# Placing the hi/lo splits of expert weights by an estimated landing time, in a two-layer decoder with a routed expert layer in each

## The chip, the core and the metric

The kernel runs on one core of one Trainium2 chip. The metric is device time in microseconds, from start to end of one launch; lower is better. The core's engines are TensorE (PE, with its weight loads as PEld), VectorE (DVE), ScalarE (ACT), GpSimd (POOL) and SyncE (SP). Each works through its own queue of instructions in order and waits on semaphores for the others. Data comes from device memory over 16 DMA engines; here SP issues nearly all of the weight loads.

## The reference, cut to what matters

A decoder trunk of two layers on one sequence of 1024 tokens, width 1024, in float32. Layer 0 mixes tokens with a gated DeltaNet, layer 1 with differential attention. After each mixer comes a layer norm and a hierarchical mixture of 32 experts, of which each token uses two:

```python
def expert_block(args):
    xb, e = args
    hcat = xb @ w13[e]
    hid = jax.nn.silu(hcat[:, :EXPERT_FF]) * hcat[:, EXPERT_FF:]
    return hid @ w2[e]

y_rows = lax.map(expert_block, (x_rows, block_eid)).reshape(n_rows, d)
y = jax.ops.segment_sum(y_rows * row_gate[:, None], row_tok, num_segments=n)
```

`w13[e]` is 1024 x 1024 and `w2[e]` 512 x 1024, so an expert has 8 + 4 weight tiles of 128 x 1024 floats, 512 KB each.

## The kernel before, in words

**Experts by rank.** After routing, the experts are ranked by how many rows they have. A table of capacities (`CAPS`) says, when the program is written, how many rows each rank gets; `blocks_of` (L1494) cuts them into blocks of at most 128 rows. `ORDER` says in which order the ranks are worked. In layer 0 large ranks (80 to 128 rows, one block) alternate with small ones (48 to 64 rows). In layer 1 a few ranks are large: rank 3 has three blocks (128, 128 and 96 rows), rank 4 three, ranks 5, 6 and 7 two each, and between them stand runs of ranks with only 16 to 32 rows.

**Two ways to multiply.** A block of at most 64 rows ("whole") multiplies the raw float32 weight tile as it is. A larger block uses three products of a high and a low part: of each weight tile, ACT makes the high part `mh` (a rounding copy) and DVE the low part `ml` (raw minus `mh`), in `cut_one` (L1426). Such a pair is called a split below; C3.0 is the split of tile 0 of rank 3. Layer 0 has 180 splits (15 ranks with 12 tiles), layer 1 has 120 (10 ranks). The matmuls of a tile need its `mh` and, from the second one on, its `ml`.

**The order of the work.** `plan` (L1500) writes out the steps of a layer: the eight tiles of the first product of a rank (`m1`), with the transposes of the next rank's rows (`trx`) and the second product of the rank before (`trh`, `m2`, and then `out`) put in between; `act` is silu times the other half. Where the next rank has three blocks, its transposes and the whole second product of the rank before it stand ahead of its first `m1`. `seq` is the order in which weight tiles are used. `experts` (L1561) walks through the steps. PE, ACT and DVE are each wrapped in `InOrder` (L202), so in each of these queues the instructions stand in the order in which `experts` writes them. A transposed group lands in PSUM (`mtr`, two buffers), and ACT and DVE empty it to `xT`, hi and lo.

**Loads.** `Weights` (L1375) keeps a ring of raw tiles, 22 in layer 0 and 20 in layer 1 (13 or 11, and 9 late ones). `load` (L1439) has SP issue loads in the order of `seq` as far as the ring goes; a slot is free again once the tile is split, or, for a tile that a small block also uses or that is not split, once its matmuls are done.

**Where a split is written.** Each `use(rank, i)` (L1474), called right in front of a tile's matmuls, writes splits for the tiles that come up in `seq`, as far as `AHEAD` = 9 tiles past the next one, at most one new one at a time, and loads in between. `cut` (L1465) stops when `room` (L1457) says that the `NHI` = 6 pairs of `mh` and `ml` are taken. Nothing asks whether a tile's load will have landed when ACT comes to its split. For rank 3 of layer 1 this gives, in front of the step m1(27.5) and around it:

```
m1(27.4) C3.0 C3.1 m2(28) out(28) C3.2
m1(27.5) C3.3
m1(27.6) trx(3, block 0) C3.4
m1(27.7) act(27) trx(3, block 1) trh(27) trx(3, block 2) C3.5 m2(27) out(27)
m1(3.0) ...
```

Ranks 4, 5 and 6 look alike: the first two to five splits of the rank stand in front of the small rank's `out` and of the emptying of the large rank's transposes.

Of the kernel before, what the change touches and what calls it, by code (L numbers as in the profile page):

```python
# [20 lines left out]
D = 1024  # L21
# [20 lines left out]

NRAW, NKEPT, NLATE, NHI, AHEAD = (13, 11), 5, 9, 6, 9
NATIVE = ((0,), ())
XB = (2, 3)
RAWA = 4
FIXED = 3
# [173 lines left out]
def mm3(c, out, ah, al, bh, bl, first, last, engine=None):  # L221
    mm = (engine or c.nc.tensor).matmul
    mm(out, ah, bh, start=first, stop=False)  # L223
    mm(out, ah, bl, start=False, stop=False)  # L224
    mm(out, al, bh, start=False, stop=last)  # L225
# [1149 lines left out]
class Weights:  # L1375
# [5 lines left out]
    def __init__(self, c, layer, kept, raw, seq):  # L1381
# [7 lines left out]
        self.loaded = self.split = self.free = self.spares = 0  # L1389
        self.cut_rows = [any(m > 64 for m in blocks_of(layer, r)) and r not in NATIVE[layer] for r, _ in seq]  # L1390
        self.held = [not cut or any(m <= 64 for m in blocks_of(layer, r)) for cut, (r, _) in zip(self.cut_rows, seq)]
# [4 lines left out]
        self.extra = NKEPT - 2 - (3 if layer == 0 else 0)  # L1396
        self.tiles, self.ids = {}, {}

    def expert(self, rank):
        if rank not in self.ids:  # L1400
            c = self.c
            self.ids[rank] = rank if rank < FIXED else c.nc.sync.value_load(
                c.eid[0:1, rank:rank + 1], min_val=0, max_val=NE - 1)
        return self.ids[rank]
# [34 lines left out]
    def load(self, upto):  # L1439
        while self.loaded < min(upto, len(self.ring)):  # L1440
            if self.late is None and self.loaded >= self.nearly:
                return
            if self.loaded >= self.nraw:
                before = self.ring[self.loaded - self.nraw]
                if before >= (self.free if self.held[before] else self.split):
                    return
            r, i = self.seq[self.ring[self.loaded]]
            self.tiles[r, i] = (self.load_one(self.expert(r), i),)
            self.loaded += 1

    def load_fixed(self):
# [13 lines left out]
    def cut(self, upto):  # L1465
        while self.split < upto and self.tiles.get(self.seq[self.split] if self.split < len(self.seq) else None):
            if self.cut_rows[self.split]:
                if not self.room():
                    return
                key = self.seq[self.split]  # L1470
                self.tiles[key] += self.cut_one(self.tiles[key][0])
            self.split += 1

    def use(self, rank, i):  # L1474

        p = self.seq.index((rank, i))
        while True:
            at = self.split
            self.load(len(self.seq))
            self.cut(min(p + 1 + AHEAD, at + 1))  # L1480
            if self.split == at:
                break
        self.load(len(self.seq))
        assert self.split > p, (rank, i)
        return self.tiles[rank, i]
# [8 lines left out]
def blocks_of(layer, rank):  # L1494


    return [min(P, CAPS[layer][rank] - q) for q in range(0, CAPS[layer][rank], P)]
# [63 lines left out]
def experts(c, layer, h_dram, y_dram):  # L1561
    nc, tc, ins, w = c.nc, c.tc, c.ins, c.w
    pe, act_, dve = (InOrder(tc, e) for e in (nc.tensor, nc.scalar, nc.vector))
    w.act, w.dve = act_, dve
    why = "expert and column numbers come from the one-hot tables made on chip"
    with ExitStack() as es:
# [7 lines left out]
        def block(xcol, ycol, rows, native=False):  # L1574
            b = B()
            b.native, b.at = native, 0
            b.xcol, b.ycol, b.rows = xcol, ycol, rows

            b.ways = 4 if rows <= 32 else 2
            b.cols = P // b.ways  # L1580
            b.whole = rows <= 64
            b.X = c.X[nx[0] % len(c.X)]
            nx[0] += 1
            c.last_gather = instruction(nc.gpsimd.indirect_dma_start(  # L1584
                out=b.X[0:rows], out_offset=None, in_=h_dram,
                in_offset=bass.IndirectOffsetOnAxis(ap=xcol[0:rows], axis=0), bounds_check=T - 1, oob_is_err=False))
            return b

        def acc():
            return ps.tile([P, 2, 512], F32, name="acc", bufs=3)  # L1590
# [19 lines left out]
        def trx(b):  # L1610

            if b.whole:
                n = b.cols
                b.x = xp.tile([P, KT, n], F32, tag="xTw", name=f"xTw{n}", bufs=3)
                pt = ps.tile([P, KT, n], F32, tag="mtr", name=f"mtw{n}")
                for k in range(KT):
                    pe.transpose(pt[:, k], b.X[0:n, k * P:(k + 1) * P], c.ident[0:n, 0:n])
                dve.tensor_copy(b.x, pt)
                return True
            if not b.at:  # L1620
                shape, dt = ([P, KT, b.rows], F32) if b.native else ([P, KT, 2 * P], F32R)
                b.x = xp.tile(shape, dt, tag="xT", name="xT", bufs=XB[layer])
            g = slice(4 * b.at, 4 * b.at + 4)
            (plain if b.native else turn)(b, b.X[:, b.at * 512:(b.at + 1) * 512], 4, b.x[:, g])
            b.at += 1
            return b.at == 2

        def product(b, out, x, wt, first, last):
            R = b.rows
            for half in range(2):  # L1630
                f = slice(half * 512, (half + 1) * 512)
                if b.native:
                    pe.matmul(out[0:R, half], x, wt[0][:, f], start=first, stop=last)
                    continue
                mm3(c, out[0:R, half], x[:, 0:R], x[:, R:2 * R], wt[1][:, f], wt[2][:, f], first, last, pe)
# [47 lines left out]

        def m1(bs, k, wt):
            for b in bs:
                if k == 0:
                    b.hc = acc()
                if not b.whole:
                    product(b, b.hc, b.x[:, k], wt, k == 0, k == KT - 1)
                    continue  # L1690

                wv = wt[0].rearrange("p (a h f) -> p h a f", a=2, h=b.ways)
                o = b.hc[:, 0, 0:D // b.ways].rearrange("p (a f) -> p a f", a=2)
                for h in range(b.ways):
                    pe.matmul(o[b.cols * h:b.cols * (h + 1)], b.x[:, k], wv[:, h], start=(k == 0), stop=(k == KT - 1))

        def m2(b, k, wt):
            if k == 0:
                b.py = acc()
            if not b.whole:  # L1700
                product(b, b.py, b.h[:, k], wt, k == 0, k == 3)
                return
            n, w = b.cols, D // b.ways
            i, g = k % (4 // b.ways), k // (4 // b.ways)
            x = b.h[:, i, n * g:n * (g + 1)]
            for f in range(b.ways):
                pe.matmul(b.py[n * f:n * (f + 1), 0, 0:w], x, wt[0][:, w * f:w * (f + 1)],
                          start=(k == 0), stop=(k == 3))

        blocks = {}  # L1710
# [1 line left out]
        def gather(n):  # L1712
            if n < len(c.jobs):
                r, rows = c.jobs[n]
                blocks[r] = [block(c.xidx[:, r * 8 + q:r * 8 + q + 1], c.yidx[:, r * 8 + q:r * 8 + q + 1], m,
                                   r in NATIVE[layer])
                             for q, m in enumerate(rows)]
# [7 lines left out]
        for what, j, k in c.steps:  # L1725
            r = j[0]
            if what == "m1":
                wt = w.use(r, k)
                m1(blocks[r], k, wt)
                w.done(r, k)  # L1730
            elif what == "trh":
                trh(blocks[r][0])
            elif what == "m2":
                bs = blocks[r]
                wts = [w.use(r, KT + i) for i in range(4)]
                for q, b in enumerate(bs):
                    for i in range(4):
                        m2(b, i, wts[i])
                        if b is bs[-1]:
                            w.done(r, KT + i)  # L1740
                        if i == 1 and q + 1 < len(bs):
                            trh(bs[q + 1])
                    out(b)
            elif what == "trx":
                for _ in range(2):
                    at = turned.get(r, 0)
                    if at < len(blocks[r]):
                        turned[r] = at + trx(blocks[r][at])
            elif what == "gather":
                gather(k)  # L1750
            else:
                for b in blocks[r]:
                    act(b)
# [11 lines left out]
        if c.overflow:  # L1765
# [3 lines left out]
            with tc.For_i(0, trips, 1) as it:  # L1769
# [8 lines left out]
                b = block(xc, yc, P)  # L1778
# [3 lines left out]
                for k in range(KT + 4):  # L1782
# [3 lines left out]
                    wt = (raws[k],) + w.cut_one(raws[k])  # L1786
# [147 lines left out]
```

## Time and profile before

| | us |
|---|---|
| median of 3 runs | 2745.63 |
| lowest and highest run | 2743.77, 2754.32 |
| the profiled execution, its own time | 2752.11 |
| its span in the trace | 2750.3 |

The profiled execution is 6.5 us above the median, inside the range of the runs; 1.8 us of it lie outside the span. Expert layer 0 takes about 800 to 1355 us of the span, expert layer 1 about 2117 to 2682 us. Busy times of engines are shares of a stretch. A matmul's end is modelled, so a busy PE is not a PE at its peak. The DMA share is the mean over 16 engines; in the busiest stretches of this trace it reads 1.03. The granted clock is a share of TensorE's full speed.

### The profile page before, as it was taken

What the parts mean: (1) busy time and instruction counts of PE and PEld (TensorE: products, weight loads), DVE (VectorE), ACT (ScalarE), POOL (GpSimd) and SP (SyncE); (2) the same over time, 40 slices, a digit from 0 to 9 for tenths busy, and PEclk for the clock granted to TensorE, in tenths of its full rate; (3) what the DMA queues carried; (4) which work ended last, traced back from release to release, by engine and by line L of the source; (5) the groups of instructions that cost most, each with busy time, mean ns of one, the idle gap of its engine ahead of it and who ended that gap; (6) DMA issues with size and microseconds to landing.
All of it is one profiled execution on the core that took longest, in us unless ns stands there. A gap on an engine that the chain in (4) does not pass through costs nothing. (4 is left out here: it accounts for less than half of the span.)

```text
span 2750.3 us, 40132 instructions
## 1 busy us (share of the span) xinstructions
PE 2366.5 (86%) x14447; PEld 1645.2 (60%) x14447; DVE 1503.0 (55%) x2710; ACT 1214.9 (44%) x2187; POOL 545.2 (20%) x445
## 2 busy tenths in 40 slices
PE   8999999998979989898649999999886796779990
PEld 5777777776745544444238777777664373455560
DVE  4555555564556555455295667667535422334467
ACT  5355555543325444444255555556332322223454
POOL 3333333331212111010042111111012111111104
PEclk9999999999979999999859999999987898899995
DMA  4111111124678999999951110101445969799995
GB/s 145 51 59 51 55 59 47 58 75 123 242 274 302 394 388 381 383 380 384 351 210 35 39 33 31 39 26 61 155 170 210 393 250 363 288 381 362 362 366 230
DMA packets 195484, 564.09 MB, mean 205 GB/s; under 512 B 40400, under 2 KB 63184, under 8 KB 193232
## 3 DMA queue, kind: packets, MB, share of 16 engines
q1 hardware_dynamic: 178240, 515.07, 51.0%
q0 software_dynamic: 15168, 43.01, 4.5%
q10 hardware_dynamic: 1872, 3.40, 0.4%
q8 instruction: 115, 1.88, 0.3%
q14 instruction: 89, 0.73, 0.1%
HBM read 515.58 MB, written 52.89 MB: 207 GB/s over the span
## 5 line engine op out<-in xcount | busy, mean ns | idle before, releaser
L210 DVE TENSOR_TENSOR ml<-mraw,mh 128x1024 fp32r<-128x1024 f32 x300 | 357.0, 1222 | 289.4 <-ACT mh L210 270.5
L210 ACT CAST mh<-mraw 128x1024 fp32r<-128x1024 f32 x300 | 306.7, 1052 | 281.7 <-DMA mraw<-in_w 226.1
L210 PE MATMUL acc<-mh,xT 128*128 128x512 f32 (+5 forms) x976 | 331.8, 409 | 1.6 <-ACT mh L210 1.6
L210 PE MATMUL acc<-mraw,xTw 128*32 128x256 f32 (+1 forms) x1632 | 241.4, 500 | 18.7 <-DVE xTw L210 10.1
L185 POOL TENSOR_TENSOR wl<-raw,wh 128x512 fp32r<-128x512 f32 x106 | 155.0, 1482 | 485.1 <-ACT wh L184 420.9
L210 PEld LDWEIGHTS acc<-mh,xT 128*128 128x128 f32 (+5 forms) x976 | 168.4, 173 | 88.3 <-issue 17.1
L223 PE MATMUL pj<-xh,wh 128*128 128x512 f32 x512 | 218.2, 426 | 0.0
L224 PE MATMUL pj<-xl,wh 128*128 128x512 f32 x512 | 209.6, 409 | 0.0
L225 PE MATMUL pj<-xh,wl 128*128 128x512 f32 x512 | 207.9, 406 | 0.4 <-POOL wl L185 0.4
L1584 POOL DMA_INDIRECT X<-h,xidx x69 | 71.0, 1029 | 651.1 <-PE mtw L210 339.0
L210 PE MATMUL acc<-ml,xT 128*128 128x512 f32 (+5 forms) x496 | 198.4, 404 | 0.8 <-DVE ml L210 0.8
L223 PE MATMUL pj<-hT,wh 128*128 128x512 f32 (+1 forms) x432 | 164.8, 381 | 9.1 <-DVE kll L1010 5.7
L224 PE MATMUL pj<-hT,wh 128*128 128x512 f32 (+1 forms) x432 | 166.9, 386 | 0.0
L225 PE MATMUL pj<-hT,wl 128*128 128x512 f32 (+1 forms) x432 | 161.2, 373 | 2.1 <-POOL wl L185 2.1
L210 PE MATMUL acc<-mh,hT 128*128 128x512 f32 (+5 forms) x480 | 158.4, 401 | 0.1
L210 PE MATMUL acc<-mraw,hTw 128*32 128x256 f32 (+1 forms) x816 | 129.3, 540 | 30.4 <-ACT hTw L210 23.9
L210 PEld LDWEIGHTS acc<-mraw,xTw 128*32 128x32 f32 (+1 forms) x1632 | 71.4, 124 | 127.8 <-issue 71.2
L408 DVE SCALAR_TENSOR_TENSOR cv<-pr,cw,cv 128x512 f32<-128x512 f32 x144 | 119.0, 826 | 51.2 <-ACT cv L405 49.1
L1114 ACT ACTIVATE e<-sc,sm 128x256 f32<-128x256 f32 (+7 forms) x128 | 94.6, 742 | 89.7 <-DVE sm L1112 89.3
L225 PEld LDWEIGHTS pj<-xh,wl 128*128 128x128 f32 x512 | 97.2, 190 | 20.1 <-POOL wl L185 0.9
L210 PEld LDWEIGHTS acc<-mh,hT 128*128 128x128 f32 (+5 forms) x480 | 82.2, 172 | 44.6 <-issue 10.5
L224 PEld LDWEIGHTS pj<-xl,wh 128*128 128x128 f32 x512 | 97.7, 191 | 18.1 <-issue 1.7
(407 smaller groups left out, 4917.7 us busy)
## 6 DMA issues: line engine op xcount, KB each, us to landing
mraw<-in_w SPq DMA_DIRECT2D x720, 512.0 KB, 10.7
raw<-in_w_in SPq DMA_DIRECT2D x32, 512.0 KB, 3.7
yin<-y SPq DMA_DIRECT2D x16, 1024.0 KB, 6.9
raw<-in_w_kvq SPq DMA_DIRECT2D x21, 512.0 KB, 3.6
h<-res SPq DMA_DIRECT2D x16, 512.0 KB, 3.9
p<-ores POOLq DMA_DIRECT2D x12, 512.0 KB, 4.8
res<-p SPq DMA_DIRECT2D x12, 512.0 KB, 5.8
mh<-in_w SPq DMA_DIRECT2D x12, 512.0 KB, 8.1
```

The source lines that it names most:

```text
L185: c.nc.gpsimd.tensor_tensor(l[:, s], src[:, s], h[:, s].bitcast(F32), OP.subtract)
L210: out = getattr(self.engine, name)(*args, **kwargs)
L223: mm(out, ah, bh, start=first, stop=False)
L224: mm(out, ah, bl, start=False, stop=False)
L225: mm(out, al, bh, start=False, stop=last)
L408: nc.vector.scalar_tensor_tensor(a, pr[:, 1 + j:513 + j], cw[:, idx, j:j + 1], a, op0=OP.mult, op1=OP.add)
L1114: nc.scalar.activation(e[:, 0:L], st[m][:, 0:L], AF.Exp, bias=sm[:, 2 + m:3 + m], scale=SC, accum_out=sm[:, 4 + m:5 + m])
L1584: c.last_gather = instruction(nc.gpsimd.indirect_dma_start(out=b.X[0:rows], out_offset=None, in_=h_dram, in_offset=bass.IndirectOffsetOnAx ...
```

## The change

`Weights` gets a clock of its own, `now`, kept while the program is written. Each matmul group of a block adds a constant (0.45, 0.9 or 1.45 by its rows, 1.7 for the one rank that multiplies natively), each transposed group 0.8. Each load gets an estimated landing time, `land`: 1.4 after the one before it, or after `now`, whichever is later. When a tile is used, `now` is moved up to its `land`. A split is then written only if its tile's estimated landing is not later than `now`, or if it is the split of the tile in use or of the next one (`must`). The loads, the ring, the six pairs and the steps stay as they are. The renaming of `w` to `z` in `m2` is needed because `w` is now read there.

```diff
+CLOAD, CSLICE, CTURN = 1.4, {32: 0.45, 64: 0.9, 128: 1.45}, 0.8
...
+        self.now = self.loads = self.must = 0
+        self.land = {}
...
             self.tiles[r, i] = (self.load_one(self.expert(r), i),)
+            if self.now:
+                self.loads = max(self.loads, self.now) + CLOAD
+            self.land[self.ring[self.loaded]] = self.loads
             self.loaded += 1
...
     def cut(self, upto):
...
-                if not self.room():
+                if not self.room() or self.split > self.must and self.land.get(self.split, 0) > self.now:
                     return
...
         p = self.seq.index((rank, i))
+        self.must = p + 1
+        self.now = max(self.now, self.land.get(p, 0))
         while True:
...
+        def cost(b):
+            return 1.7 if b.native else CSLICE[32 if b.rows <= 32 else 64 if b.rows <= 64 else 128]
...
         def m1(bs, k, wt):
             for b in bs:
+                w.now += cost(b)
...
         def m2(b, k, wt):
+            w.now += cost(b)
...
-            n, w = b.cols, D // b.ways
+            n, z = b.cols, D // b.ways
...
                     if at < len(blocks[r]):
+                        w.now += CTURN
                         turned[r] = at + trx(blocks[r][at])
```

Followed through by hand, the new rule leaves 156 of the 300 splits where they were, writes 144 later (92 in layer 0, all among ranks 7 to 15; 52 in layer 1, among ranks 3 to 7) and none earlier. For rank 3 of layer 1 it gives:

```
m1(27.4) m2(28) out(28)
m1(27.5)
m1(27.6) trx(3, block 0)
m1(27.7) act(27) trx(3, block 1) trh(27) trx(3, block 2) C3.0 m2(27) out(27) C3.1
m1(3.0) C3.2 C3.3 ...
```

Rank 4 is the same. For rank 5 the splits C5.0 and C5.1 now stand behind all of its transposes, in front of m1(19.6), and for rank 6 C6.0 in front of m1(16.7).

## Rows read from the trace of the kernel before

**Rows 1.** Stages: us; busy PE, PEld, DVE, ACT, POOL (count); clock, DMA share, GB/s.

```profile
850.00:1350.00 500.00, 455.68 (x2076) 239.13 (x2073) 258.53 (x279) 212.79 (x277) 60.30 (x55) 0.97 1.02 384
...
2220.00:2280.00 60.00, 58.44 (x463) 40.35 (x461) 14.55 (x23) 11.96 (x21) 7.79 (x8) 1.00 0.60 222
2320.00:2380.00 60.00, 60.00 (x387) 36.81 (x383) 14.89 (x21) 13.15 (x21) 5.78 (x6) 0.98 0.66 235
2400.00:2460.00 60.00, 57.08 (x471) 40.31 (x472) 20.36 (x30) 16.29 (x28) 7.80 (x8) 0.94 0.99 378
2480.00:2660.00 180.00, 177.83 (x847) 107.05 (x846) 99.07 (x107) 82.24 (x107) 20.44 (x18) 1.00 0.98 374
```

**Rows 2.** Waits, 2080 to 2700 us: total us, times, longest.

```profile
PE mtr L210 <- DVE xT L210: 52.1, 4, 14.5
...
ACT mh L210 <- DMA mraw<-in_w: 70.9, 22, 17.2
```

**Rows 3.** First stall, timeline: start, us, engine, line, operation, tiles, count [idle before <-releaser].

```profile
2186.60 1.08 PE L210 MATMUL acc<-mraw,xTw 128*32 128x256 f32 x8
...
2191.35 1.04 ACT L210 CAST mh<-mraw 128x1024 fp32r<-128x1024 f32 x1 [17.24 <-DMA mraw<-in_w]
2192.42 1.23 DVE L210 TENSOR_TENSOR ml<-mraw,mh 128x1024 fp32r<-128x1024 f32 x1 [19.85 <-ACT mh L210]
...
2197.85 1.07 ACT L210 CAST xT<-mtr 128x512 fp32r<-128x512 f32 x2
...
2200.05 1.97 PE L210 MATMUL mtr<-ct_all,X 128*128 128x128 f32 x8 [12.37 <-DVE xT L210]
...
2208.51 0.80 PE L210 MATMUL acc<-mh,xT 128*128 128x512 f32 x1
```

**Rows 4.** Stages: the four stalls, from the last matmul before to the next transposes.

```profile
2187.68:2200.05 12.37, 0.00 (x1) 0.00 (x1) 6.40 (x8) 6.81 (x10) 1.03 (x2) 0.50 1.03 403
2299.33:2312.75 13.42, 0.00 (x0) 0.00 (x1) 6.40 (x8) 6.81 (x10) 1.47 (x2) 0.59 1.03 402
2390.90:2402.72 11.82, 0.01 (x2) 0.00 (x0) 7.71 (x9) 6.93 (x9) 1.23 (x2) 0.62 1.03 398
2461.64:2476.10 14.46, 0.00 (x1) 0.00 (x1) 7.72 (x9) 6.93 (x9) 1.74 (x3) 0.63 1.03 408
```

**Rows 5.** Timeline, stalls two to four: the rank's first split and its first matmul.

```profile
2304.24 1.04 ACT L210 CAST mh<-mraw 128x1024 fp32r<-128x1024 f32 x1 [16.61 <-DMA mraw<-in_w]
...
2320.78 0.80 PE L210 MATMUL acc<-mh,xT 128*128 128x512 f32 x1
...
2392.42 1.04 ACT L210 CAST mh<-mraw 128x1024 fp32r<-128x1024 f32 x1 [9.49 <-DMA mraw<-in_w]
...
2406.49 0.80 PE L210 MATMUL acc<-mh,xT 128*128 128x512 f32 x1
...
2464.87 1.04 ACT L210 CAST mh<-mraw 128x1024 fp32r<-128x1024 f32 x1 [7.68 <-DMA mraw<-in_w]
...
2479.43 0.50 PE L210 MATMUL acc<-mh,xT 128*128 128x512 f32 x1
```

**Rows 6.** Timeline, end of layer 1: last weight loads, a late split, last matmuls.

```profile
2561.66 97.99 SPq L1423 DMA_DIRECT2D mraw<-in_w  x70
...
2590.96 1.05 ACT L210 CAST mh<-mraw 128x1024 fp32r<-128x1024 f32 x1 [3.46 <-DMA mraw<-in_w]
...
2680.20 1.93 PE L210 MATMUL acc<-mraw,hTw 128*32 128x256 f32 x32 [0.35 <-ACT hTw L210]
```

**Rows 7.** Layer 0, 1050 to 1300 us: DMA issues (KB, us to landing), then SP's waits.

```profile
mraw<-in_w SPq DMA_DIRECT2D x168, 512.0 KB, 12.0
...
SPq L1423 <- DMA mraw<-in_w: 156.9, 168, 2.7
```

**Rows 8.** Timeline, end of layer 0: last weight loads, last matmuls.

```profile
1331.61 12.69 SPq L1423 DMA_DIRECT2D mraw<-in_w  x10
...
1351.97 3.76 PE L210 MATMUL acc<-mraw,hTw 128*64 128x512 f32 x16 [0.52 <-ACT hTw L210]
```

More of the change, by code (lines that the diff above doesn't have):

```diff
@@ L1706, in m2 @@
             for f in range(b.ways):
-                pe.matmul(b.py[n * f:n * (f + 1), 0, 0:w], x, wt[0][:, w * f:w * (f + 1)],
+                pe.matmul(b.py[n * f:n * (f + 1), 0, 0:z], x, wt[0][:, z * f:z * (f + 1)],
                           start=(k == 0), stop=(k == 3))
```

## The prediction, made before the changed kernel had run

> **What bounds the kernel now.** I read the profile page first. Its slices show DMA and TensorE both near full in the two expert layers, so the page does not say which of them a split can hold up; the change moves nothing outside those layers. So I cut them into stages.
>
> Layer 0 is bound by DMA: from 850 to 1350 us the DMA share is 1.02 without a break [rows 1]. SP issued 168 weight loads in 250 us of that stretch, and in front of 168 it waited for an earlier load, not for a free ring slot [rows 7]. The layer also ends with its loads: the last ten were issued between 1331.6 and 1344.3 us, a load takes 12.0 us to land, and the last matmuls start at 1352.0 [rows 7, 8].
>
> Layer 1 changes its bound from stage to stage. While ranks 3 and 4 are multiplied, PE is full and the DMA share falls to 0.60 and 0.66, because loads wait for PE to free slots; from 2400 to 2460 us DMA is at 0.99; from 2480 to 2660 both are nearly full [rows 1].
>
> Then the waits. In layer 1, PE waited four times, 52.1 us together, for DVE to empty `mtr` into `xT` [rows 2]. The timeline of the first stall shows why: ACT stood 17.24 us in front of C3.0, whose load landed at 2191.35, and the `xT` copies, whose input had been in PSUM since about 2186.6, came behind it in ACT's queue, at 2197.85. PE went on at 2200.05 [rows 3]. The four stalls last 12.37, 13.42, 11.82 and 14.46 us, 52.07 in all, which is the wait's total; in each, PE does nothing and DMA runs at 1.03 [rows 4].
>
> **The change, part by part.** It removes and adds no instruction: 300 casts, 300 subtractions and all loads stay. SP's loads keep their order; POOL's queue holds no split. What moves are 144 splits, one ACT and one DVE instruction each, later in those two queues. The estimate itself costs the chip nothing, since it runs while the program is written.
>
> Layer 0: 92 splits move, all among ranks 7 to 15. I count 0. What hides them is the DMA stream: with the share at 1.02, an earlier matmul only meets a load that has not landed, and the last three ranks have no splits, so the end stays tied to the last load. If a late split held a ring slot too long, loads would be late next; the slower rival prices that. The bounds are a gain of 3 us (the last matmuls against the last landing give no more [rows 7, 8]) and that loss.
>
> Layer 1, stalls: with C3.0 behind the emptying of rank 3's transposes, PE can start the next transposes when the first ones are emptied. From the first `xT` cast to PE's next transposes took 2.2 us in the trace; about 1.1 of it lies beside the small rank's last matmuls (1.08 us) [rows 3]. So I leave 1.0 us of each stall. What PE did from the end of a stall to the large rank's first matmul stays, at the same durations, as the granted clock is low there either way (0.50 to 0.63, so mostly at 1.2 GHz) [rows 4]. But that matmul also needs its split: landing plus 1.04 on ACT plus 1.23 on DVE, some 2.3 us [rows 3]. The four first matmuls [rows 3 to 5]:
>
> - Rank 3: 2187.68 + 1.0 + (2208.51 - 2200.05) = 2197.1; the split allows 2193.7. 11.4 us earlier.
> - Rank 4: 2299.33 + 1.0 + (2320.78 - 2312.75) = 2308.4; the split allows 2306.5. 12.4 us earlier.
> - Rank 5: 2390.90 + 1.0 + (2406.49 - 2402.72) = 2395.7; the split allows 2394.7. 10.8 us earlier.
> - Rank 6: 2461.64 + 1.0 + (2479.43 - 2476.10) = 2466.0; the split allows 2467.2. 12.2 us earlier.
>
> How much of that reaches the end depends on DMA. A gain on PE lasts only if the loads behind it come earlier too, and they do where DMA had gaps that a slot freed earlier closes. With 1.03 as full, the gaps are 60 x (1 - 0.60/1.03) = 25 us behind stall 1, 22 behind stall 2, 2.3 behind stall 3 and 180 x (1 - 0.98/1.03) = 8.7 behind stall 4 [rows 1]. So stalls 1 and 2 count in full, 11.4 and 12.4. Stall 3 counts 2.3, since PE just reaches the next unlanded load sooner. For stall 4 PE is the bound to the end: loads ended at 2659.7 plus some 12 us of landing, the last matmuls start at 2680.2 [rows 6, 7]. It has 8.7 us of gaps plus that lead of some 8 us, more than 12.2. Against it, the splits of ranks 8 to 11 do not move, and one there already waited 3.46 us for its load [rows 6]; with PE earlier, such waits grow. Between 8.7 (gaps alone) and 12.2 I take 10.
>
> New waits: a large rank's splits now come one or two tiles ahead instead of up to nine. Its loads follow each other faster than PE uses tiles of two or three blocks, and PE is full in these stages [rows 1]; a split takes 2.3 us in two engines that are at most 55% busy there. I count 0, at worst one split per moved rank, 5 x 2.3 = 11.5 us in layer 1. Behind a split that still waits on ACT stand the small rank's `out` copies and its silu; only the accumulators wait for those.
>
> Sum: 11.4 + 12.4 + 2.3 + 10 = 36.1 us. The profiled execution took 2752.1 us, 6.5 above the median; 2752.1 becomes 2716.0, and the median 2745.6 becomes 2709.5.
>
> **A rule against it.** The trace shows DMA at 1.03 in all four stalls [rows 4]. The Trainium skill, page Perfetto Trace Analysis, section Identifying the Most-Contended Engine, says that the engine (or memory traffic) with the highest use in a regime is the one to work on first. Applied to the stalls, that is DMA, which this change does not touch, and the sum would be 0. My sum goes by the stage behind each stall instead, where DMA falls to 0.60 and 0.66 [rows 1], and so counts full stalls only there.
>
> **Rivals.**
>
> *A: the wait only changes its name.* PE would wait for the loads themselves. For it: DMA is full in every stall. Against it: C3.0's load had landed 17 us before rank 3's first matmul [rows 3], and DMA has gaps soon after. It would give at most stall 3's kind of gain once, 2.3 us: 2743.3. This is also where the page's rule leads.
>
> *B: the estimate is too early.* The change then does only part of what it says: where `land` runs ahead of the real landings, splits again stand in front of copies that could go first. For ranks 3 and 4 the rule puts no split ahead of the transposes, whatever the real landing, so stalls 1 and 2 go anyway. For ranks 5 to 7 it rests on the estimate. With stalls 1 and 2 alone: 2745.6 - 23.8 = 2721.8.
>
> *C, slower: late splits keep ring slots.* Place: ranks 8 to 15 of layer 0, with the small ranks between them 192 loads at 250/168 = 1.49 us, 286 us [rows 7]. A slot of the 22 must be free 22 x 1.49 = 32.7 us after its issue, or 20.7 after landing. Moved splits come at most 11 tile steps later, 16.4 us, so this should not bite. If a slot were held 24 us, the ring would turn in 36 us instead of 32.7: 10% of 286, 29 us. Layer 1's ring is two slots smaller and its gain would go the same way: 2745.6 + 29 = 2775. It decides from 20.7 us between landing and split.
>
> **How the numbers follow.** About 0.5%, 13.7 us, is what a measurement of this kernel can tell from no change. My forecast has 0.71; it lies between 24 us of gain with some loss and all four stalls in full (46.8 us, 2698.8). B has 0.15, A 0.09, C 0.05. Faster takes the forecast and B: 0.86. Same is A: 0.09. Slower is C: 0.05. The range goes from 2697, all four stalls and 2 us of layer 0, to 2732, B with 10 us of new split waits. A and C lie outside it, 14 in 100.
>
> **What would show it.** Right: in the changed kernel's layer 1 the wait of PE's `mtr` for DVE's `xT` falls from 52 us to under 8; ACT's casts wait for loads less than the 70.9 us of before [rows 2]; rank 3's first matmul comes about 11 us and rank 4's about 24 us earlier, counted from the start of layer 1; DMA's stages at 0.60 and 0.66 come sooner and are shorter. Layer 0 keeps its length within 3 us and its DMA share of 1.02. Wrong: the same 50 us appear as waits of PE's matmuls for `mraw` loads (A); stalls 3 and 4 remain (B); SP waits for DVE or PE instead of earlier loads in layer 0 and the DMA share falls under 1 (C).

## The result, and the profile after

The changed kernel took 2703.53 us (median of 4 runs, 2701.77 to 2706.94) against 2746.6 us (4 runs) for the kernel before: ratio 0.9842, 95% interval 0.9828 to 0.9855. That is 43.1 us less; the prediction had 36.1 less and a range of 2697 to 2732.

The two profiled executions differ by 45.2 us of span. Cut at the first and last matmul of each expert layer (first-matmul times of the timeline, subtracted):

| part of the span, us | before | after | difference |
|---|---|---|---|
| up to layer 0's first expert matmul | 801.5 | 800.2 | -1.3 |
| layer 0, first to last expert matmul | 550.5 | 545.6 | -4.8 |
| between the layers | 765.6 | 767.0 | +1.3 |
| layer 1, first to last expert matmul | 562.6 | 522.0 | -40.6 |
| behind it | 70.1 | 70.3 | +0.2 |

Layer 1 is where the time came from. Its waits in the changed kernel, 2080 to 2720 us (total us, times, longest), to be held against [rows 2]:

```profile
ACT mh L212 <- DMA mraw<-in_w: 46.4, 32, 7.2
...
PE acc L212 <- DMA mraw<-in_w: 16.4, 28, 1.8
...
PE acc L212 <- DVE ml L212: 2.8, 4, 0.8
...
PE mtr L212 <- DVE xT L212: 1.6, 3, 1.1
```

The wait of `mtr` for `xT` is gone (52.1 us before, 1.6 now). It did not become a wait for loads: PE's matmuls waited 14.8 us for `mraw` in the same stretch of the kernel before and wait 16.4 us now. ACT still waits for loads, more often but shortly (7.2 us at the longest, 17.2 before), and PE waited only 1.7 us for a high part.

The place of the first stall, timeline of the changed kernel, the counterpart of [rows 3]:

```profile
2182.13 1.08 PE L212 MATMUL acc<-mraw,xTw 128*32 128x256 f32 x8
...
2183.14 1.74 PE L212 MATMUL mtr<-ct_all,X 128*128 128x128 f32 x8
...
2187.73 1.06 ACT L212 CAST mh<-mraw 128x1024 fp32r<-128x1024 f32 x1
...
2189.08 0.49 PE L212 MATMUL acc<-mh,xT 128*128 128x512 f32 x1
```

The transposes now follow the small rank's last matmuls at once, where PE stood 12.37 us before [rows 4]. The split (2187.73) stands behind all emptying and finds its load landed: no idle time is noted in front of it. The next first matmuls and the last matmuls:

```profile
2112.83 1.97 PE L212 MATMUL acc<-mh,xTw 128*64 128x512 f32 x4 [0.78 <-DVE xTw L212]
...
2285.06 1.05 ACT L212 CAST mh<-mraw 128x1024 fp32r<-128x1024 f32 x1 [1.51 <-DMA mraw<-in_w]
...
2286.16 0.51 PE L212 MATMUL acc<-mh,xT 128*128 128x512 f32 x1
...
2359.57 0.51 PE L212 MATMUL acc<-mh,xT 128*128 128x512 f32 x1 [1.18 <-ACT mh L212]
...
2430.80 0.50 PE L212 MATMUL acc<-mh,xT 128*128 128x512 f32 x1 [0.57 <-ACT mh L212]
...
2634.85 1.93 PE L212 MATMUL acc<-mraw,hTw 128*32 128x256 f32 x32 [0.35 <-ACT hTw L212]
```

The first row is the layer's first matmul, from which everything below is counted (before, it stood at 2117.59); then come the first matmuls of ranks 4, 5 and 6. At rank 4 the split waited 1.51 us for its load, at ranks 5 and 6 PE waited 1.18 and 0.57 us for the split: the first loads of these ranks are the next limit. The stages of the changed kernel (columns as in [rows 1]):

```profile
2183.14:2189.08 5.94, 4.75 (x54) 3.28 (x50) 3.29 (x7) 3.52 (x7) 2.04 (x3) 0.88 1.03 400
2220.00:2260.00 40.00, 38.69 (x368) 25.54 (x366) 9.42 (x18) 7.74 (x17) 6.76 (x7) 1.00 0.75 277
2300.00:2340.00 40.00, 40.00 (x236) 24.95 (x238) 10.73 (x14) 9.06 (x13) 4.00 (x4) 1.00 0.81 311
2340.00:2620.00 280.00, 263.15 (x1580) 159.66 (x1576) 139.76 (x162) 118.51 (x165) 36.72 (x35) 0.98 1.02 396
...
850.00:1350.00 500.00, 455.03 (x2072) 232.18 (x2070) 256.82 (x278) 212.76 (x278) 63.06 (x55) 0.99 1.02 384
```

The second and third rows hold the gaps of DMA behind stalls 1 and 2: 0.75 and 0.81 over 40 us, against 0.60 and 0.66 over 60 us before [rows 1]. Read in steps of 10 us, DMA stood below 0.95 from 2220 to 2270 and from 2320 to 2380 us, and now does so only between 2220 and 2250 and between 2320 and 2340. From 2340 us on it is full. The queue that issues loads says the same. SP's waits, 2080 to 2720 us, before:

```profile
SPq L1423 <- PE acc L210: 183.9, 103, 15.8
SPq L1423 <- DMA mraw<-in_w: 161.6, 186, 3.5
```

and after:

```profile
SPq L1428 <- DMA mraw<-in_w: 234.4, 260, 2.8
SPq L1428 <- PE acc L212: 79.7, 64, 14.2
```

Loads that waited for PE to free a slot now wait for the loads ahead of them. In layer 0 (last row of the stages) nothing of the kind moved: DMA share 1.02 as before.

### The profile page after: what moved, and what is told of

Same layout as the page of the kernel before. It is cut to its first block, busy times and chain, and to the rows that moved or that the text cites. A ratio compares the mean times of both kernels' runs of the same rounds, so it can differ in the third digit from the quotient of the medians.

```text
span 2705.1 us, 40128 instructions
## 1 busy us (share of the span) xinstructions
PE 2366.5 (87%) x14447; PEld 1636.9 (61%) x14447; DVE 1503.5 (56%) x2710; ACT 1214.4 (45%) x2187; POOL 548.1 (20%) x445
## 5 line engine op out<-in xcount | busy, mean ns | idle before, releaser
L212 PE MATMUL acc<-mraw,hTw 128*32 128x256 f32 (+1 forms) x816 | 122.7, 515 | 13.9 <-ACT hTw L212 7.2
L212 PEld LDWEIGHTS acc<-ml,xT 128*128 128x128 f32 (+5 forms) x496 | 84.9, 171 | 52.7 <-DVE ml L212 25.4
L212 PEld LDWEIGHTS acc<-mh,hT 128*128 128x128 f32 (+5 forms) x480 | 82.3, 173 | 54.8 <-ACT mh L212 12.4
```

The source lines that it names most:

```text
L212: out = getattr(self.engine, name)(*args, **kwargs)
```

## The experiments

Each is the changed kernel with one edit to the condition in `cut` (and `self.layer` kept for it), or a kernel with one constant changed. Below, g stands for `self.split > self.must and self.land.get(self.split, 0) > self.now`. Ratios are against the kernel before, run beside them, with 95% intervals. "L1" is layer 1 from its first to its last matmul (562.6 us before, 522.0 after), "rank 3 at" the first matmul of rank 3 counted from the same start, from one profiled execution each.

**One layer alone.** The rule is applied in layer 1 only, then in layer 0 only.

```diff
-                if not self.room() or g:
+                if not self.room() or self.layer == 1 and g:
```

> The estimate gates splits in layer 1 alone; layer 0 is as in the kernel before. Theory (the gain is the four stalls of layer 1; the 6 us by which layer 0 ended earlier in the trace of the changed kernel come from a higher granted clock in its first 60 us, before any moved split, and not from the change): as fast as the changed kernel within 3 us, 2701 to 2707, ratio to before 0.983 to 0.986. Rival (layer 0's 92 moved splits give some 6 us): 2708 to 2711.

2702.3 us, ratio 0.9836 [0.9822, 0.9851]; L1 521.8.

```diff
+                if not self.room() or self.layer == 0 and g:
```

> The estimate gates splits in layer 0 alone; layer 1 is as in the kernel before. Theory: no change, within 3 us of the kernel before, 2743 to 2750, ratio 0.999 to 1.001. Rival (layer 0 gains): 2739 to 2742, ratio 0.998 or less.

2746.35 us, ratio 1.0 [0.999, 1.0009]; L1 563.2. Its wait of `mtr` in layer 1:

```profile
PE mtr L212 <- DVE xT L212: 54.7, 4, 15.0
```

Layer 1 alone gives all of the gain; the 92 splits moved in layer 0 give nothing. The 4.8 us by which layer 0 was shorter in the profile after are not the rule's: the second kernel, with the rule in layer 0, needs 550.5 us there as before; the first, without it, 546.7. What went along with the length was the granted clock in the layer's first 60 us: before,

```profile
800.00:860.00 60.00, 57.51 (x204) 32.12 (x205) 29.80 (x31) 28.82 (x36) 7.03 (x6) 0.89 0.59 206
```

the rule in layer 0 only,

```profile
800.00:860.00 60.00, 57.54 (x206) 31.49 (x206) 32.03 (x33) 30.07 (x37) 9.07 (x6) 0.91 0.59 208
```

the rule in layer 1 only,

```profile
800.00:860.00 60.00, 56.77 (x223) 29.77 (x221) 34.76 (x37) 31.39 (x39) 11.13 (x5) 0.99 0.62 221
```

and 0.98 in the profile after. Two executions with a clock of 0.89 and 0.91 took 550.5 us, two with 0.98 and 0.99 took 545.6 and 546.7. Five kernels below agree, at 0.97 to 1.00 in these 60 us and 545.0 to 547.4 for the layer: the one with four splits put back has the rule in layer 0 (1.00, 545.4 us), the one for ranks 3 and 4 alone has not (1.00, 545.4 us). So a single profile's layer 0 is uncertain by 5 us, and parts of layer 1 are compared by L1.

**Stalls 1 and 2 alone**, the rule for ranks 3 and 4 of layer 1 (18 splits moved):

```diff
+                if not self.room() or self.layer == 1 and self.seq[self.split][0] in (3, 4) and g:
```

> Only splits of ranks 3 and 4 of layer 1 are gated, 18 of the 144 moves. Theory (stalls 1 and 2 count in full, some 15 us each with the clock kept up; stalls 3 and 4 stay): gain 27 to 31, 2715 to 2720. Rival A2 (DMA sets the pace of the whole layer, so whichever stall goes the loads behind it take the gain back): gain under 10, above 2736. Rival B2 (the gain goes with the number of moved splits): 18 of 52, some 14 us, 2732.

2714.43 us, ratio 0.9887 [0.9866, 0.9907]; L1 533.7, 28.9 shorter. Rank 3 starts at 76.3 and rank 4 at 174.2, as in the changed kernel (76.2, 173.3), and the other two stalls are left:

```profile
PE mtr L212 <- DVE xT L212: 27.2, 2, 15.1
```

So stalls 1 and 2 count in full to the layer's end. The step from here to all four is 533.7 - 522.0 = 11.7 us.

**Four splits put back**, of the 144: C3.0, C4.0, C5.0 and C6.0 stand early again.

```diff
+                if not self.room() or not (self.layer == 1 and
+                        self.seq[self.split] in ((3, 0), (4, 0), (5, 0), (6, 0))) and g:
```

> As the changed kernel, but the first split of ranks 3, 4, 5 and 6 in layer 1 stands where it stood before, in front of the copies: 4 of the 144 moves undone. Theory (one split that waits for its load holds up all the copies behind it in the queue): PE waits again for the emptying of mtr in front of each of the four ranks, till the load has landed, some 8 us at ranks 3 and 4 and 5 to 7 at ranks 5 and 6; 16 to 23 us slower than the changed kernel, 2719 to 2727. Rival B2 (the gain goes with the number of moved splits): 4 of 52, 3 us slower, 2707.

2724.48 us, ratio 0.9924 [0.9907, 0.9941]: half of the gain is gone. The stalls are back with the chain that the prediction read from [rows 3]; timeline of the first one:

```profile
2175.47 0.64 PE L212 MATMUL acc<-mraw,xTw 128*32 128x256 f32 x8
...
2180.37 1.04 ACT L212 CAST mh<-mraw 128x1024 fp32r<-128x1024 f32 x1 [16.70 <-DMA mraw<-in_w]
...
2183.55 1.07 ACT L212 CAST xT<-mtr 128x512 fp32r<-128x512 f32 x2
...
2184.91 1.97 PE L212 MATMUL mtr<-ct_all,X 128*128 128x128 f32 x8 [8.80 <-DVE xT L212]
...
2192.88 0.50 PE L212 MATMUL acc<-mh,xT 128*128 128x512 f32 x1
```

and its stages, the stall and the way from there to rank 3's first matmul:

```profile
2175.47:2184.91 9.44, 0.64 (x9) 0.16 (x8) 2.81 (x5) 2.93 (x6) 1.55 (x2) 0.67 1.03 403
2184.91:2192.88 7.97, 7.01 (x50) 4.31 (x50) 3.24 (x6) 2.40 (x5) 2.01 (x3) 0.54 1.03 400
```

ACT stands 16.70 us in front of one cast of 1.04 us, with the emptying behind it in its queue, and PE stands 8.80 us. The four stalls last 8.80, 10.29, 7.53 and 7.39 us, shorter than before: here the `xT` copies of rank 3 follow 2.1 us after the end of C3.0's cast, where three more casts stood between and made it 5.5 us [rows 3]. In first matmuls, C3.0 alone brings back 9.6 of the 14.7 us gained at rank 3 (85.8 against 76.2), C4.0 alone 10.9 of 15.2. Behind the stall the same work takes 7.97 us at a granted clock of 0.54, against 5.94 us at 0.88 in the changed kernel.

**Ranks 5 and 6 one by one**, to weigh stalls 3 and 4:

```diff
+                if not self.room() or self.layer == 1 and self.seq[self.split][0] == 5 and g:
```

> Only the 12 splits of rank 5 in layer 1 are gated, so only stall 3 goes. Theory (behind stall 3 DMA has no gaps, so the loads of rank 6 land hardly sooner): rank 5's first matmul 10 to 13 us sooner after the start of layer 1, rank 6's and the layer's end only 0 to 4: 2741 to 2747. Rival (a stall on PE counts in full wherever it is): the end 10 to 13 us sooner, 2733 to 2736.

2744.16 us, ratio 0.9999 [0.9989, 1.0008]; L1 559.9. Rank 5 starts 12.3 us earlier (276.6 against 288.9), rank 6 only 1.7 (360.1 against 361.8), the end 2.7. From rank 5's first matmul to rank 6's:

```profile
2382.45:2465.95 83.50, 63.52 (x484) 40.81 (x484) 31.52 (x39) 25.62 (x38) 11.57 (x12) 0.86 1.03 400
```

DMA is at 1.03 all the way, and stall 4 is still in this kernel. It ends with C6.0's load, whose cast starts 345.6 us into the layer where it had been 347.3: the load had no gap to come earlier through. PE does not reach the stall sooner either (344.5 us into the layer, 344.1 before). From rank 5's first matmul to there, this kernel and then the kernel before:

```profile
2382.45:2450.34 67.89, 59.94 (x459) 38.78 (x459) 22.02 (x28) 17.64 (x27) 9.35 (x10) 0.92 1.03 398
```

```profile
2406.49:2461.64 55.15, 54.58 (x463) 38.69 (x459) 16.36 (x23) 13.68 (x23) 6.73 (x7) 0.99 0.98 374
```

The 12.3 us went into waits (8.0 us idle where it had been 0.6, half of it for loads) and into the same matmuls at a lower granted clock. By the median of its runs this kernel can't be told from the kernel before, so 2.7 us is the reading of one execution.

```diff
+                if not self.room() or self.layer == 1 and self.seq[self.split][0] == 6 and g:
```

> Only the 12 splits of rank 6 in layer 1 are gated, so only stall 4 goes. Theory (PE is the bound from there to the end of the layer, with loads some 8 us and DMA gaps of 8.7 us in hand): rank 6's first matmul 12 to 14 us sooner and the layer's end 8 to 12: 2734 to 2738. Rival (DMA is the bound behind stall 4 too): the end 0 to 4 us sooner, 2742 to 2746.

2738.72 us, ratio 0.9973 [0.9964, 0.9983]; L1 555.3, 7.3 shorter, a little under what was expected. Rank 6 starts 12.6 us earlier, rank 7 only 6.5. Between the two DMA is full and PE waits 5.4 us in four small waits,

```profile
2462.21:2528.00 65.79, 61.41 (x299) 36.72 (x299) 29.61 (x33) 22.76 (x31) 9.77 (x10) 0.96 1.03 399
```

where the kernel before took 59.7 us, with PE busy for 58.35 at a clock of 1.00. The longest of the waits is at rank 7, whose splits are not gated in this kernel and stand in front of its emptying:

```profile
2524.57 0.71 PE L212 MATMUL mtw<-ct_all,X 64*128 64x64 f32 x8 [2.58 <-DVE xT L212]
```

In the changed kernel, where rank 7 is gated too, the same stretch takes 60.8 us, also with DMA at 1.03. So a full DMA alone does not explain what was lost here. From rank 7 on nothing more is lost (6.5 and 7.3 are within the reading). Alone, the two stalls are worth 2.7 + 7.3 = 10.0 us, together 11.7.

**Is the estimate needed, or only lateness?** First without it: a split is written only for the tile in use and the next one, 298 moved.

```diff
+                if not self.room() or self.split > self.must:
```

> The estimate is left out: a split is written only for the tile in use and the next one, in both layers; 298 of the 300 splits then stand later than in the kernel before. Theory (what counts is that no split stands ahead of a large rank's transposes; earlier splits elsewhere only serve the lead over PE): the four stalls are gone, layer 1 within 5 us of the changed kernel; splits one tile ahead may cost PE up to 2.3 us at each large rank: 2703 to 2718. Rival E (the estimate itself earns the gain, since splits too late starve PE: 2.3 us of split latency at most of the 120 tiles of layer 1): over 2730.

2735.48 us, ratio 0.9959 [0.9944, 0.9974]: the theory's range is missed by 17 us, and the rival's side (over 2730) came out. The stalls are gone here too; two other things cost what they gave. PE waits for the low parts, in layer 0 and in layer 1 (780 to 1380, 2080 to 2720 us):

```profile
PE acc L212 <- DVE ml L212: 42.9, 59, 1.0
...
PE acc L212 <- DVE ml L212: 19.9, 27, 0.8
```

against 17.9 us in 23 and 2.8 in 4 in the changed kernel. L1 is 539.0, 17 longer than after. And at the start of layer 0 slots come free later:

```profile
800.00:860.00 60.00, 52.92 (x183) 27.87 (x182) 25.65 (x26) 23.63 (x31) 3.93 (x4) 0.93 0.52 169
```

The DMA share there is 0.52 where 0.59 stood before and 0.63 in the changed kernel. SP waited once for 20.8 us for DVE's `ml` there (13.4 at the longest in the changed kernel). In the first 80 us of the layer it issued 31 weight loads, in the changed kernel 40 and before 37:

```profile
mraw<-in_w SPq DMA_DIRECT2D x31, 512.0 KB, 5.5
```

```profile
mraw<-in_w SPq DMA_DIRECT2D x40, 512.0 KB, 8.3
```

At 1.49 us for a load, the pace of the full stream [rows 7], 9 or 6 loads are 13.4 or 8.9 us, and the layer took 559.9 us, 14.3 more than after and 9.4 more than before. In all, SP waited 87.6 us for `ml` in the layer (37.5 in the changed kernel), but most of the difference lies behind its first 80 us, where the DMA share is at 1.02 all the same. This is rival C's mechanism, a split that keeps a ring slot, in another place: at the start of the layer, where the loads do not yet run at full share.

Then fixed distances, the kernel before with 2 or 4 tiles in place of 9 and no estimate:

```diff
-NRAW, NKEPT, NLATE, NHI, AHEAD = (13, 11), 5, 9, 6, 9
+NRAW, NKEPT, NLATE, NHI, AHEAD = (13, 11), 5, 9, 6, 2
```

> The kernel before with one number changed, AHEAD from 9 to 2, and no estimate. C3.0 and C4.0 then stand behind all transposes of their rank, C5.0 and C6.0 too. Theory: the four stalls are gone and the lead is one tile more than in the run without the estimate: 2701 to 2712. Rival E (the estimate earns the gain): over 2720.

2711.4 us, ratio 0.9877 [0.9848, 0.9906]; L1 527.2. The four stalls are gone; PE waits 7.9 us in 11 for `ml` in layer 1 and 24.4 in 34 in layer 0.

```diff
+NRAW, NKEPT, NLATE, NHI, AHEAD = (13, 11), 5, 9, 6, 4
```

> The kernel before with AHEAD 4. C3.0 and C4.0 stand behind all transposes of their rank, but C5.0 and C6.0 in front of the small rank's out and of their own rank's transposes. Theory: stalls 1 and 2 go, 3 and 4 come back at the price of one split ahead, as where the first split was put back: layer 1 gains 30 to 36, 2710 to 2718. Rival E: over 2725.

2720.91 us, ratio 0.9921 [0.9891, 0.9952]; L1 536.3, gaining 26.3 where 30 to 36 was expected. Stalls 1 and 2 are gone and stalls 3 and 4 are back, at 6.2 and 7.6 us, as expected; beside that, rank 4 starts 5.9 us later than in the changed kernel (179.2 against 173.3) without a stall in front of it. The third blocks of ranks 3 and 4 wait 2.4 and 2.5 us for `yw`, the small rank's `out` copies, which here stand behind four splits of the large rank, so accumulators come free later. The wait of `mtr`:

```profile
PE mtr L210 <- DVE xT L210: 14.3, 3, 7.6
```

Last, the estimate moved to either side, a load taken for 1.0 or 1.8 us instead of 1.4:

```diff
-CLOAD, CSLICE, CTURN = 1.4, {32: 0.45, 64: 0.9, 128: 1.45}, 0.8
+CLOAD, CSLICE, CTURN = 1.0, {32: 0.45, 64: 0.9, 128: 1.45}, 0.8
```

> The changed kernel with an estimate that is too early: 1.0 instead of 1.4 for a load. 22 splits of layer 1 then stand later than in the kernel before and none of layer 0. C3.0 stands between the emptying of block 0 and of block 1, C5.0 and C6.0 in front of the small rank's out, as before. Theory (rival B of the prediction with its cause set on purpose): stalls 3 and 4 come back, stalls 1 and 2 by a third to a half: gain 15 to 25, 2721 to 2731. Rival (the landing time that is assumed hardly matters): 2703 to 2710.

2720.7 us, ratio 0.9903 [0.9883, 0.9922]; L1 535.7. The time is at the edge of what was expected, with other stalls than were named: 3 and 4 are back, at 8.7 and 7.1 us, stall 1 by more than a half (7.2 us, in front of the small rank's `mtw` transposes), and stall 2 is not.

```profile
PE mtr L212 <- DVE xT L212: 16.2, 3, 8.7
...
PE mtw L212 <- DVE xT L212: 9.3, 3, 7.2
```

```diff
+CLOAD, CSLICE, CTURN = 1.8, {32: 0.45, 64: 0.9, 128: 1.45}, 0.8
```

> The changed kernel with an estimate that is too late: 1.8 instead of 1.4 for a load. 139 splits of layer 0 and 103 of layer 1 then stand later than in the kernel before. Theory (too late costs PE waits for splits, as without the estimate, but the four stalls stay away): layer 1 some 5 to 12 us longer than in the changed kernel, layer 0 up to 5: 2708 to 2722. Rival (later is no worse, as long as no split stands ahead of the transposes): 2700 to 2706.

2713.81 us, ratio 0.9891 [0.9875, 0.9908]; L1 529.0. No stalls, but in layer 1

```profile
PE acc L212 <- DVE ml L212: 11.4, 16, 0.8
```

Too early by 0.4 us a load costs layer 1 13.7 us, too late by as much 7.0 us.

## Why the prediction was right, point by point

**The mechanism was right.** An early split in front of the emptying of transposes made the stalls: all 144 moves take them away, four undone bring them back, shorter. The signs named came as said: `mtr`'s wait under 8 us, ACT's waits for loads 46.4 instead of 70.9, the low DMA stages shorter, layer 0's share at 1.02. Ranks 3 and 4 came 14.7 and 29.9 us earlier, more than the 11 and 24 named. Two signs fell out otherwise. Layer 0 was 4.8 us shorter where 3 was allowed, which is not the rule's. And the low DMA stages begin no sooner, 107 and 207 us into layer 1 where it had been 102 and 202: ahead of them DMA is at 1.03 either way, so the loads there end when they did.

**The terms.** First matmuls from the start of layer 1, in us; "step gained" is what was gained since the row above:

| | before | after | step gained | local shift forecast | counted |
|---|---|---|---|---|---|
| rank 3 | 90.9 | 76.2 | 14.7 | 11.4 | 11.4 |
| rank 4 | 203.2 | 173.3 | 15.2 | 12.4 | 12.4 |
| rank 5 | 288.9 | 246.7 | 12.3 | 10.8 | 2.3 |
| rank 6 | 361.8 | 318.0 | 1.6 | 12.2 | 10 |
| last matmul | 562.6 | 522.0 | -3.2 | | |
| sum | | | 40.6 | | 36.1 |

**Ranks 3 and 4 were sized too small, by 3.3 and 2.8 us.** Two steps of the working failed. "What PE did from the end of a stall to the large rank's first matmul stays, at the same durations, as the granted clock is low there either way": it does not. For rank 3 this took 5.94 us at a granted clock of 0.88 where it had been 8.46 us (in the kernel before the profile shows 0.50 for it, the 1.2 GHz level, all the way); for rank 4 it is 5.35 us at 1.00 instead of 8.03 at 0.50. In both cases PE no longer stands still ahead of it; that the clock follows from this is read from these stages and was not tested by itself. The two stages before, and rank 4's after (rank 3's is shown above):

```profile
2200.05:2208.51 8.46, 7.49 (x49) 4.39 (x49) 5.51 (x8) 3.35 (x7) 1.78 (x2) 0.50 1.03 392
2312.75:2320.78 8.03, 7.06 (x49) 4.06 (x50) 4.99 (x7) 2.38 (x5) 2.03 (x2) 0.50 1.03 396
```

```profile
2280.81:2286.16 5.35, 4.19 (x50) 2.48 (x50) 2.98 (x6) 2.81 (x6) 2.63 (x3) 1.00 1.03 391
```

And of "1.0 us of each stall" nothing is left: PE ends its small matmuls at 2183.2 and starts the transposes at 2183.14. For rank 3, 11.4 + 2.5 + 1.0 = 14.9, measured 14.7. For rank 4, 12.4 + 2.7 + 1.0 = 16.1, measured 15.2, so 0.9 us of it is not accounted for. The kernel with four splits put back shows the pair again (7.97 us at 0.54).

**Ranks 5 and 6 were right in sum, not each.** Counted 2.3 + 10 = 12.3 at the end; the step from ranks 3 and 4 alone to all gives 11.7. That the two agree so well is in part luck: alone the stalls gave 2.7 and 7.3, together 1.7 more. The reason given for stall 3 held alone (counted 2.3, read 2.7: DMA without gaps). With all four gone the gain stands at rank 5 and is missing at rank 6, and 3.2 us are given back behind it, where DMA is full; the forecast kept 10 of 12.2 for such losses, and rank 6 alone kept 7.3 of 12.6, in part because rank 7's own splits then stood in the way.

**Layer 0 at 0** was right, by the kernel with the rule there alone. **New waits at 0** was right too (2.8 us in four waits, mostly small), but only for splits as late as the estimate puts them: with splits just in front of the use PE waited 19.9 us for low parts in layer 1. In layer 0 it waited 17.9 us for them in the changed kernel too, and that cost nothing, as the layer goes by its loads.

**The rivals.** A fell: no wait took the place of the stalls. The rule that goes with it is in the Trainium skill, page Perfetto Trace Analysis, section Identifying the Most-Contended Engine: the most-contended engine is the one to work on first. As the prediction applied it to the stalls, this change would give nothing. The same section of the Trainium skill judges DMA by its memory traffic, not by the busy share of the DMA engines. The prediction went by the share; in this case both point the same way, as the traffic in the stalls was 398 to 408 GB/s [rows 4], against 222 and 235 behind stalls 1 and 2 [rows 1]. The runs divide the rule as the prediction applied it: it holds behind stall 3, where DMA stays at 1.03 and removing a stall gave at most some 3 us, and fails for stalls 1 and 2, behind which DMA had gaps and 28.9 us were gained. B did not happen, as 1.6 us of wait show, but it was a real danger: with loads taken for 1.0 us splits stand in front of copies again and the kernel lands at 2720.7. That this is close to B's price (2721.8) is luck: B left stalls 3 and 4 as they were and took 1 and 2 away, and here stall 1 is back by more than a half and stalls 3 and 4 are shorter. C did not happen with the estimate, and did at the start of layer 0 without it.

**What stays open:** which of the moved splits beside the first one of each rank matter. Four put back cost 21 us of 43; for the other half the record shows only the further casts in front of the emptying, at rank 3. Whether some fixed distance, 3 tiles say, does as well as the estimate was not tried: with 2 tiles the interval of the ratio (0.9848 to 0.9906) still meets that of the estimate (0.9828 to 0.9855). Nor was the cause of the differing clock at the start of layer 0 looked for.

## What to carry to other kernels

In an engine's in-order queue, an operation that waits for a load must not stand ahead of work that another engine needs sooner: look for a long wait of a cheap operation (17.24 us in front of a 1.04 us cast) and read what stands behind it. Place it as late as its load needs and no later: here 9 tiles ahead cost 43 us against the estimate, 4 tiles 17, 2 tiles 8 (hardly clear of noise), and a split just in front of its use 32, because lateness has its own price in waits for the result and in buffers kept. Whether a stall taken away counts at the end is read from the stage behind it, by whether transfers have gaps there to be drawn into.

## What the runs showed of the hardware

The time of a stall is not all that a stall costs. Behind 9 to 13 us of standing still, PE's next transposes and small matmuls ran at granted clocks of 0.50 to 0.54 and took 8.0 to 8.5 us; without the stall they ran at 0.88 and 1.00 and took 5.4 to 5.9 us, some 2.5 us more gained for each of stalls 1 and 2. The granted clock also differs between executions without a change of program there: 0.89 in the kernel before and 0.99 with the rule in layer 1 only, in the first 60 us of layer 0, and 550.5 and 546.7 us for its length.
